# Moving eight U chunks from the one-hot table into the routing stage, and ending the expert gathers before the last V chunks

## The chip, the cores and the metric

One NeuronCore of a Trainium2 chip runs the whole layer in one launch. The metric is the device time of one execution in microseconds; the time before is the median of three runs. The engines are TensorE (PE, its weight loads shown as PEld), VectorE (DVE), ScalarE (ACT), GpSimd (POOL) and SyncE (SP), which only issues DMAs here.

## The reference, cut to what matters

The layer is attention plus a gated recurrence, followed by a product-key expert layer (PEER) and a last RMSNorm, for 512 tokens of width 1024. Nearly all of the change lies in PEER:

```python
sc = einsum('bshpd,phnd->bshpn', q, keys)          # 8 heads, 2 key halves, 128 keys each
v1, i1 = top_k(sc[..., 0, :], 16); v2, i2 = top_k(sc[..., 1, :], 16)
cand = v1[..., :, None] + v2[..., None, :]          # 256 candidates per head
best, pos = top_k(cand, 16); idx = take(i1 * 128 + i2, pos)   # 16 experts of 16384 per head
gates = softmax(best)
act = gelu(einsum('tkd,td->tk', u[idx], h))         # u, v: (16384, 1024)
out = einsum('tk,tkd->td', gates * act, v[idx])
```

## The kernel before, in words

The experts are done in two ways. For 352 tokens (`DT`) the kernel does not gather: it computes all 16384 activations and outputs densely, as 128 chunks of 128 experts. A **U chunk** (`act_pieces`, L629 on) loads 512 KB of `u`, splits it on ACT into `hi` (L142) and on DVE into `lo` (L162) so that two fast fp32 products replace a slow one, and does 24 matmuls of 352 columns (L646); ACT writes `gelu` of it to one of 53 held tiles (`KEEP`). A **V chunk** (the loop `for c in range(NE)` near the end) loads 512 KB of `v`, splits it likewise, multiplies the held tile by the gates (`w`, L980; `whi`, `wlo`, L985) and adds 18 matmuls of 512 columns (L994 to L996) to six accumulators. The other 160 tokens are done sparsely: 320 **gather steps** (128 for 128 tokens of block 0 with `u`, 32 and 32 for the other 32 tokens, 128 with `v`). Each is an indirect DMA issued by POOL (L707), 128 rows of 1024 floats into one of four tiles (`GB`), and one DVE instruction on it (L715 for `u`, L725 for `v`).

The stages after the front part are these.

1. **Routing.** Sixteen key halves (`hp`). Each loads its weights `wq` and keys, projects (24 matmuls of 512 columns), forms scores (L847) and takes the best 16 on DVE; every second one also runs `route` on DVE. `fill(int(F1 * (hp + 1)) - int(F1 * hp))` puts U chunks between the halves: with `F1 = 1.5` one and two in turn, 24 in all. Two more follow the routing.
2. **Table.** The gates must be spread to a dense table `G` of 128 x 128 experts by 352 tokens. For 22 slices of 16 tokens, DVE builds one-hot tiles `oh` (L904 to L907, two buffers), PE multiplies them (L912, 8 matmuls per group of 4 tokens, 88 groups), ACT copies out (L914) and issues the write to DRAM (L916, 1 MB per slice). After each group one quarter of a U chunk is put on PE (`piece`), until 48 chunks are held. `pace(goal, after)` issues gathers up to `goal` and puts the DVE step that lies three behind (`GLAG`) after the instruction named.
3. **Hold.** Three U chunks, two V loads, the first read of the table (`g_load`, which must wait for the last table write), nine gathers up to number 16 (`EARLY`), two U chunks.
4. **Loop.** 128 V chunks, the remaining 75 U chunks spread over the first 116 (`UEND`), and the remaining 304 gather steps, spread in proportion to the chunks done (`share`). Near the end `final_rows` adds the parts, normalises and writes out; block 0 of the tokens (`ys[0]`) is done after the loop.

The order on each engine is chosen by the tile scheduler from the order of the program, its priorities and the `issue_after` hints; POOL's gathers and the table's matmuls keep program order.

Of the kernel before, what the change touches and what calls it, by code (L numbers as in the profile page):

```python
# [6 lines left out]
F32 = mybir.dt.float32  # L7
# [5 lines left out]
OP = mybir.AluOpType  # L13
# [33 lines left out]
VPRE = 2  # L47
GLAG = 3
GB = 4
TAILC = 2  # L50
HELD = 5
LASTU = 2
EARLY = 16
UEND = 116
TL = 2
F1 = 1.5


def host(inp):
# [57 lines left out]
def layer(nc, tc, a, out, probe=None, upto=99):  # L117
# [37 lines left out]
    def wsplit(raw, shape, parts=1, eng=None):  # L155
        hi = oc.tile(list(shape), F32R, tag="hi", bufs=HB, name=nm("hi"))
        lo = oc.tile(list(shape), F32R, tag="lo", bufs=HB, name=nm("lo"))
        n = shape[1] // parts
        for i in range(parts):
            m = slice(i * n, (i + 1) * n)  # L160
            hi_of(hi[:, m], raw[:, m])
            (eng or V).tensor_tensor(lo[:, m], raw[:, m], hi[:, m].bitcast(F32), op=OP.subtract)  # L162
        return hi, lo


# [455 lines left out]
    with tc.tile_pool(name="peer", bufs=1) as pp, tc.tile_pool(name="psp", bufs=1, space=PSUM) as psp, ExitStack() as ps:  # L621
# [7 lines left out]
        def gel_tile(c):  # L629
            i = c % KEEP  # L630
            if i < LOOK:
                return pp.tile([P, DT], F32, tag="gel", bufs=LOOK, name=nm("gel"))
            if i < LOOK + LATE:
                return cur["gel2"].tile([P, DT], F32, tag="gel2", bufs=LATE, name=nm("gel"))
            return extra[i - LOOK - LATE]


        def act_pieces(c, pin=False):
# [237 lines left out]
        with tc.tile_pool(name="gb", bufs=1, reuse_waits="tile") as gp:  # L876
            iT = gp.tile([P, 2, DT], F16, name="iT")
            gs = gp.tile([P, DT], F32, name="gs")
            g16 = gp.tile([P, 2, DT], F16, name="g16")
            fill(2)  # L880
            for n in range(1, NB):
                f = X if n == 1 else 0
                t = slice((n - 1) * P - X + f, n * P - X)
                b = bank((P, 4, P))
                for w in range(2):
                    PE.transpose(b[:, w, :], i12[:, w, n, :], ident)
                PE.transpose(b[:, 2, :], gta[:, n, :], ident)
                ACT.activation(iT[:, :, t], b[:, 0:2, f:], AF.Copy)
                ACT.activation(gs[:, t], b[:, 2, f:], AF.Copy, scale=GS)  # L889
                V.tensor_copy(g16[:, 0, t], gs[:, t])  # L890
                V.tensor_tensor(g16[:, 1, t], gs[:, t], g16[:, 0, t], op=OP.subtract)
            NQ = OT // QT
            shape = [P, NQ, P, QT]
            for s_ in range(NPT):
                G_ = gp.tile([P, NE, TG], F32, tag="G", bufs=2, name=nm("G"))
                for o in range(TG // OT):
                    t = slice(s_ * TG + o * OT, s_ * TG + (o + 1) * OT)

                    def row(x):
                        return x.rearrange("p (q t) -> p q t", t=QT).unsqueeze(2).to_broadcast(shape)  # L900

                    ioq = iok.unsqueeze(1).to_broadcast(shape)
                    oh = gp.tile([P, 3, NQ, P, QT], F16, tag="oh", bufs=2, name=nm("oh"))
                    V.tensor_tensor(oh[:, 0], ioq, row(iT[:, 0, t]), op=OP.is_equal)  # L904
                    V.tensor_tensor(oh[:, 2], ioq, row(iT[:, 1, t]), op=OP.is_equal)
                    V.tensor_tensor(oh[:, 1], oh[:, 2], row(g16[:, 0, t]), op=OP.mult)
                    last = V.tensor_tensor(oh[:, 2], oh[:, 2], row(g16[:, 1, t]), op=OP.mult)  # L907
                    for q in range(NQ):
                        b = bank((P, QT, P))
                        for i in range(QT):  # L910
                            for w in range(2):
                                lastg = tc.keep_in_program_order(PE.matmul(b[:, i, :], oh[:, 0, q, :, i], oh[:, 1 + w, q, :, i], start=w == 0, stop=w == 1))  # L912
                        m = o * OT + q * QT
                        ACT.activation(G_[:, :, m:m + QT].rearrange("p c t -> p t c"), b, AF.Copy)  # L914
                        piece(KEEP - HELD)
                ACT.dma_start(Gd.rearrange("g p s f -> s p g f")[s_], G_.rearrange("p (g c) t -> p g (c t)", c=GC))  # L916
                pace((s_ + 1) // 3, last.ins)
        late = ps.enter_context(tc.tile_pool(name="late", bufs=1, reuse_waits="tile"))
# [17 lines left out]
                return SP.dma_start(gts[g], Gd[g])  # L936

        with tc.issue_after(lastg.ins):
            fill(KEEP - nu[0] - LASTU)
        for c in range(VPRE):  # L940
            v_load(c)
        g0 = g_load(0)
        pace(EARLY, last.ins)
        with tc.issue_after(lastg.ins), tc.issue_after(g0.ins):
            fill(LASTU)

# [22 lines left out]

        todo_u = NE - nu[0]  # L970
        nu0 = nu[0]
        ready = []
        for c in range(NE):
            if c % GC == 0:
# [38 lines left out]
            if c == NE - 6:  # L1013
# [4 lines left out]
                    bs.append(bank(tag="p"))  # L1018
                    PE.matmul(bs[hf][0:X, :], fold[:, 0:X], sp1.ax[:, hf * 512:(hf + 1) * 512], start=True, stop=True)
                final_rows(yx[0:X, :], [b[0:X, :] for b in bs], P, X)  # L1020
            pace(EARLY + (NS - EARLY) * share, last.ins)

        while nsp[0] < NS:
            sparse(nsp[0])
            nsp[0] += 1
        final_rows(ys[0], [sp0.ax[:, 0:512], sp0.ax[:, 512:]], 0, P)
        for n in range(DB):
            m = min(P, DT - n * P)
            final_rows(ys[n + 1][0:m, :], [acc[n][hf][0:m, :] for hf in range(2)], T0 + n * P, m)
# [17 lines left out]
```

## Time and profile before

| | before |
|---|---|
| median of 3 runs | 1669.36 us (1662.62 to 1670.48) |
| the profiled execution | 1675.46 us, its span 1673.7 us |
| PE busy | 1605.2 us (96%) |
| DVE busy | 1321.9 us (79%) |
| ACT, POOL busy | 709.6 us (42%), 487.3 us (29%) |
| moved by DMA | 400.87 MB, mean 240 GB/s |

The profiled execution was 6.1 us longer than the median of the timed runs. Busy shares are averages over stages with different limits, so they say little here: the stages are read one by one, from the stretches in the section of rows. A row of the timeline is start, duration, engine, line, operation, output and inputs; a bracket at its end tells how long the engine sat idle before it and what released it. A row of the stretches gives for each engine the busy time and the number of instructions, then TensorE's granted clock as a share of 2.4 GHz, the busy share of the 16 DMA engines and the rate.

### The profile page before, as it was taken

The numbers are of one execution on the slowest core, as the hardware profiler recorded it, in microseconds if no ns is written. First come the engines' busy times: TensorE is split into PE (matmuls) and PEld (weight loads), VectorE is DVE, ScalarE is ACT, GpSimd is POOL, SyncE is SP. The second block draws the span as 40 slices with busy tenths as digits, with TensorE's granted clock in tenths as the row PEclk, the third lists the DMA queues.
The fourth block names the chain that finished last, engine by engine and source line by source line (L and its number), as shares of the span: only waits on it lengthen the run. The fifth ranks groups of instructions, "written<-read, shape, count | busy, mean of one in ns | idle before, by whom it ended". The sixth has DMA issues, their size and how long they took to land.

```text
span 1673.7 us, 23435 instructions
## 1 busy us (share of the span) xinstructions
PE 1605.2 (96%) x8511; PEld 1358.7 (81%) x8511; DVE 1321.9 (79%) x2560; ACT 709.6 (42%) x1152; POOL 487.3 (29%) x341
## 2 busy tenths in 40 slices
PE   8999999999999969997899999999999999999996
PEld 6877678888988869997788888887888888888874
DVE  8456663647999988887688888878888888888887
ACT  5433353234554547775333333333333333333333
POOL 4000000000000010002455555445455555554542
PEclk9999999999999979999899999999999999999998
DMA  5311133334333347888999999999999999999984
GB/s 173 101 51 51 51 104 111 103 115 154 108 109 116 103 126 192 219 224 265 336 340 353 349 368 349 337 341 339 344 368 351 359 354 347 360 358 363 343 305 145
DMA packets 197491, 400.87 MB, mean 240 GB/s; under 512 B 103344, under 2 KB 105904, under 8 KB 197376
## 3 DMA queue, kind: packets, MB, share of 16 engines
q1 hardware_dynamic: 58832, 206.02, 35.2%
q0 software_dynamic: 46336, 168.39, 27.0%
q10 hardware_dynamic: 92208, 24.98, 6.1%
q8 instruction: 66, 1.08, 0.3%
q14 instruction: 49, 0.40, 0.1%
HBM read 371.91 MB, written 27.39 MB: 239 GB/s over the span
## 4 chain that ended last, share of the span: by engine, by line
PE 53%; issue 16%; POOL 12%; DVE 12%; DMA 6%; ACT 1%; POOLq 0%; DVEq 0%; SPq 0%; ACTq 0%
PE b L646 13%; POOL ga L707 11%; PE b L263 5%; PE b L262 5%; PE b L995 5%; PE b L996 5%; PE b L265 4%; PE b L994 4%; DMA ga<-v,idx 4%; PE b L912 4%; DVE lo L162 3%; DMA ga<-un,idx 1%; DVE ti L858 1%; DVE mr L856 1%; DVE e L725 1%
## 5 line engine op out<-in xcount | busy, mean ns | idle before, releaser
L707 POOL DMA_INDIRECT ga<-un,idx x160 | 225.2, 1407 | 944.5 <-ACT gs L889 581.3
L646 PE MATMUL b<-hT,hi 128*128 128x352 f32 x2048 | 366.9, 327 | 2.2 <-ACT hi L142 1.7
L646 PEld LDWEIGHTS b<-hT,hi 128*128 128x128 f32 x2048 | 334.4, 190 | 12.7 <-ACT hi L142 2.0
L995 PE MATMUL b<-lo,whi 128*128 128x512 f32 (+1 forms) x768 | 305.0, 397 | 15.0 <-DVE lo L162 14.6
L996 PE MATMUL b<-hi,wlo 128*128 128x512 f32 (+1 forms) x768 | 304.3, 396 | 0.0
L994 PE MATMUL b<-hi,whi 128*128 128x512 f32 (+1 forms) x768 | 302.7, 395 | 0.0
L707 POOL DMA_INDIRECT ga<-v,idx x160 | 240.4, 1502 | 208.3 <-DVE e L725 190.3
L142 ACT ACTIVATE hi<-s 128x1024 fp32r<-128x1024 f32 (+1 forms) x195 | 205.1, 1052 | 203.1 <-PE b L646 88.1
L162 DVE TENSOR_TENSOR lo<-s,hi 128x1024 fp32r<-128x1024 f32 (+1 forms) x195 | 238.5, 1224 | 29.7 <-ACT hi L142 28.0
L142 ACT ACTIVATE whi<-w 128x352 fp32r<-128x352 f32 x128 | 63.7, 498 | 400.0 <-PE b L995 361.2
L725 DVE SCALAR_TENSOR_TENSOR e<-ga,wt,e 128x1024 f32<-128x1024 f32 x158 | 202.2, 1280 | 19.3 <-DMA ga<-v,idx 18.4
L715 DVE SCALAR_TENSOR_TENSOR ga<-ga,h 128x1024 f32<-128x1024 f32 x160 | 194.5, 1220 | 28.6 <-DMA ga<-un,idx 26.9
L646 PE MATMUL b<-hT,lo 128*128 128x352 f32 x1024 | 191.3, 325 | 11.8 <-DVE lo L162 11.8
L995 PEld LDWEIGHTS b<-lo,whi 128*128 128x128 f32 (+1 forms) x768 | 138.8, 181 | 59.2 <-DVE lo L162 22.0
L646 PEld LDWEIGHTS b<-hT,lo 128*128 128x128 f32 x1024 | 168.0, 189 | 12.4 <-DVE lo L162 12.3
L996 PEld LDWEIGHTS b<-hi,wlo 128*128 128x128 f32 (+1 forms) x768 | 138.5, 180 | 39.3
L994 PEld LDWEIGHTS b<-hi,whi 128*128 128x128 f32 (+1 forms) x768 | 138.2, 180 | 35.3 <-ACT hi L142 1.2
L142 ACT ACTIVATE hi<-vr 128x1024 fp32r<-128x1024 f32 x128 | 134.6, 1051 | 75.9 <-PE b L646 46.3
L162 DVE TENSOR_TENSOR lo<-vr,hi 128x1024 fp32r<-128x1024 f32 x128 | 156.1, 1220 | 9.4 <-ACT hi L142 9.4
L263 PE MATMUL b<-hT,hi 128*128 128x512 f32 (+1 forms) x376 | 146.4, 391 | 0.3 <-DVE hT L145 0.3
L262 PE MATMUL b<-hT,hi 128*128 128x512 f32 (+1 forms) x376 | 146.1, 390 | 0.2
L985 DVE TENSOR_TENSOR wlo<-w,whi 128x352 fp32r<-128x352 f32 x128 | 67.0, 523 | 80.9 <-ACT whi L142 77.5
(284 smaller groups left out, 1960.5 us busy)
## 6 DMA issues: line engine op xcount, KB each, us to landing
s<-uc SPq DMA_DIRECT2D x128, 512.0 KB
vr<-vc SPq DMA_DIRECT2D x128, 512.0 KB
Gd<-G ACTq DMA_DIRECT2D x22, 1024.0 KB
gt<-Gd SPq DMA_DIRECT2D x32, 704.0 KB
s<-wfm SPq DMA_DIRECT2D x30, 512.0 KB
s<-wq SPq DMA_DIRECT2D x16, 512.0 KB
s<-wmg SPq DMA_DIRECT2D x8, 512.0 KB
s<-wout SPq DMA_DIRECT2D x8, 512.0 KB
```

The source lines that it names most:

```text
L142: ACT.activation(dst, src, AF.Copy)
L162: (eng or V).tensor_tensor(lo[:, m], raw[:, m], hi[:, m].bitcast(F32), op=OP.subtract)
L262: PE.matmul(b, wh[:, k, :], rh(i), start=start and i == 0, stop=False)
L263: PE.matmul(b, wh[:, k, :], rl(i), start=False, stop=False)
L646: m = PE.matmul(o, w[:, k, :], z[:, k, t], start=i == 0, stop=i == 3 * KD - 1)
L707: tc.keep_in_program_order(POOL.indirect_dma_start(out=t, out_offset=None, in_=a[src], in_offset=bass.IndirectOffsetOnAxis(ap=b.idx[:, j:j ...
L715: V.scalar_tensor_tensor(t, t, 1.0, h20, op0=OP.mult, op1=OP.mult, accum_out=b.act[:, j:j + 1])
L725: V.scalar_tensor_tensor(b.ax, t, b.wt[:, j:j + 1], b.ax, op0=OP.mult, op1=OP.add)
L985: last = V.tensor_tensor(wlo, w, whi.bitcast(F32), op=OP.subtract)
L994: PE.matmul(acc[tb][hf][0:m, :], whi[:, t], vh[:, d], start=i == 0, stop=False)
L995: PE.matmul(acc[tb][hf][0:m, :], whi[:, t], vl[:, d], start=False, stop=False)
L996: PE.matmul(acc[tb][hf][0:m, :], wlo[:, t], vh[:, d], start=False, stop=i == NE - 1)
```

## The change

Five constants and statements change. `F1 = 2.0` puts two U chunks behind every key half (32 instead of 24); so 34 are done when the table begins, and its 14 remaining chunks (56 quarters) are spread evenly over the 88 groups. The held tiles are taken in another order, since more of them are needed before the pool of the last 17 opens. In the hold, each of the three U chunks brings one gather, whose DVE step is put behind that chunk's `lo`; the burst up to number 16 goes, so the loop begins with 10 gathers issued and has 310 to issue. `TAILC = 8` makes `share` reach 1 at V chunk 119 (counted from 0) instead of 125, and the last steps and the end of block 0 are put into the loop at chunk 123.

```diff
-TAILC = 2
+TAILC = 8
-EARLY = 16
-F1 = 1.5
+F1 = 2.0
...
-            (eng or V).tensor_tensor(lo[:, m], raw[:, m], hi[:, m].bitcast(F32), op=OP.subtract)
+            cur["lo"] = (eng or V).tensor_tensor(lo[:, m], raw[:, m], hi[:, m].bitcast(F32), op=OP.subtract)
...
-            if i < LOOK + LATE:
-                return cur["gel2"].tile([P, DT], F32, tag="gel2", bufs=LATE, name=nm("gel"))
-            return extra[i - LOOK - LATE]
+            if i < LOOK + E8S:
+                return extra[i - LOOK]
+            return cur["gel2"].tile([P, DT], F32, tag="gel2", bufs=LATE, name=nm("gel"))
...
+            NPT_B = DT // QT
+            npc = 4 * (KEEP - HELD - nu[0])
...
-                        piece(KEEP - HELD)
+                        k = (s_ * TG + m) // QT
+                        if (k + 1) * npc // NPT_B > k * npc // NPT_B:
+                            piece(KEEP - HELD)
...
         with tc.issue_after(lastg.ins):
-            fill(KEEP - nu[0] - LASTU)
+            for _ in range(KEEP - nu[0] - LASTU):
+                fill(1)
+                pace(nga[0] + 1, cur["lo"].ins)
...
-        pace(EARLY, last.ins)
...
+        e0 = nga[0]
...
-            pace(EARLY + (NS - EARLY) * share, last.ins)
-
-        while nsp[0] < NS:
-            sparse(nsp[0])
-            nsp[0] += 1
-        final_rows(ys[0], [sp0.ax[:, 0:512], sp0.ax[:, 512:]], 0, P)
+            if c == NE - 5:
+                while nsp[0] < NS:
+                    sparse(nsp[0])
+                    nsp[0] += 1
+                final_rows(ys[0], [sp0.ax[:, 0:512], sp0.ax[:, 512:]], 0, P)
+            pace(e0 + (NS - e0) * share, last.ins)
```

How the order of instructions moves is shown at three places. Lines of the changed kernel lie a few off those before (L162 is L161 there, L715 is L714, L725 is L724, L960 is L964).

SP in the middle of the routing, which issues the loads of the keys (`ky`), the projection weights (`wq`) and the U chunks (`uc`). Before:

```order
L836 DMA ky_3902<-keys 128x128
L152 DMA s_660_3788<-uc 128x1024
L152 DMA s_665_3821<-uc 128x1024
L836 DMA ky_4052<-keys 128x128
L152 DMA s_682_3904<-wq 128x1024
L870 DMA gate_3082<-gta 32x32
L152 DMA s_688_3942<-uc 128x1024
L836 DMA ky_4206<-keys 128x128
```

Now:

```order
L835 DMA ky_3847<-keys 128x128
L151 DMA s_634_3666<-wq 128x1024
L151 DMA s_640_3704<-uc 128x1024
L151 DMA s_645_3737<-uc 128x1024
L835 DMA ky_4001<-keys 128x128
L151 DMA s_669_3849<-wq 128x1024
L151 DMA s_675_3887<-uc 128x1024
L151 DMA s_680_3920<-uc 128x1024
```

Between two loads of keys there stand one and two U chunks in turn before, and always two now.

DVE at the end of the table and in the hold, from the last one-hot tiles to the first weighted tile `w` of the loop (`ga` is a gathered tile, `act` its sums). Before:

```order
L907 TENSOR_TENSOR oh_7456<-oh_7456,g_5521 128x1024
L715 SCALAR_TENSOR_TENSOR ga_6902,act_3079<-ga_6902,h_62 128x1024
...
L162 TENSOR_TENSOR lo_7349<-s_1252_7346,hi_7348 128x1024
L715 SCALAR_TENSOR_TENSOR ga_7609,act_3079<-ga_7609,h_62 128x1024
...
L715 SCALAR_TENSOR_TENSOR ga_7624,act_3079<-ga_7624,h_62 128x1024
L162 TENSOR_TENSOR lo_7510<-s_1275_7507,hi_7509 128x1024
L162 TENSOR_TENSOR lo_7542<-s_1279_7539,hi_7541 128x1024
L162 TENSOR_TENSOR lo_7574<-s_1283_7571,hi_7573 128x1024
L980 SCALAR_TENSOR_TENSOR w_7708<-gel_3136,gt_7607 128x352
```

Now:

```order
L908 TENSOR_TENSOR oh_7450<-oh_7450,g_5779 128x1024
L161 TENSOR_TENSOR lo_7505<-s_1270_7502,hi_7504 128x1024
L714 SCALAR_TENSOR_TENSOR ga_6977,act_3079<-ga_6977,h_62 128x1024
L161 TENSOR_TENSOR lo_7541<-s_1276_7538,hi_7540 128x1024
L714 SCALAR_TENSOR_TENSOR ga_7196,act_3079<-ga_7196,h_62 128x1024
L161 TENSOR_TENSOR lo_7577<-s_1282_7574,hi_7576 128x1024
L714 SCALAR_TENSOR_TENSOR ga_7415,act_3079<-ga_7415,h_62 128x1024
L985 SCALAR_TENSOR_TENSOR w_7690<-gel_3136,gt_7614 128x352
```

The `...` stand for two and four more gather steps. Nine of them stood before the three held `lo`; now each `lo` comes first and one step follows it.

DVE at the end of the loop (`e_528` holds block 0's sums, `vr` is a raw V chunk). Before:

```order
L725 SCALAR_TENSOR_TENSOR e_528_3077<-ga_14917,wt_3080,e_528_3077 128x1024
L162 TENSOR_TENSOR lo_14957<-vr_14887,hi_14956 128x1024
L985 TENSOR_TENSOR wlo_14964<-w_14960,whi_14962 128x352
L725 SCALAR_TENSOR_TENSOR e_528_3077<-ga_14920,wt_3080,e_528_3077 128x1024
L985 TENSOR_TENSOR wlo_14974<-w_14970,whi_14972 128x352
L725 SCALAR_TENSOR_TENSOR e_528_3077<-ga_14953,wt_3080,e_528_3077 128x1024
L162 TENSOR_TENSOR lo_14967<-vr_14923,hi_14966 128x1024
L960 TENSOR_TENSOR e_2724_14751<-e_2724_14751,e_528_3077 128x512 x2
```

Now:

```order
L724 SCALAR_TENSOR_TENSOR e_528_3077<-ga_14709,wt_3080,e_528_3077 128x1024
L724 SCALAR_TENSOR_TENSOR e_528_3077<-ga_14742,wt_3080,e_528_3077 128x1024
L161 TENSOR_TENSOR lo_14790<-vr_14712,hi_14789 128x1024
L990 TENSOR_TENSOR wlo_14797<-w_14793,whi_14795 128x352
L964 TENSOR_TENSOR e_2733_14778<-e_2733_14778,e_528_3077 128x512
L985 SCALAR_TENSOR_TENSOR w_14872<-gel_14196,gt_14605 128x352
L964 TENSOR_TENSOR e_2733_14778<-e_2733_14778,e_528_3077 128x512
```

The last gather step stood before the `lo` of the very last V chunk; now seven `lo` of V chunks come after it.

## Rows read from the trace of the kernel before

**Rows 1.** The stretches: routing, table, hold, loop, end; times from the span's start.

```profile
391.60:580.30 188.70, 184.37 (x1014) 166.64 (x1013) 177.99 (x883) 102.43 (x224) 0.00 (x0) 1.00 0.35 116
611.50:783.30 171.80, 169.60 (x1227) 156.84 (x1226) 146.39 (x209) 118.65 (x128) 12.72 (x9) 0.99 0.78 213
783.30:818.67 35.37, 22.90 (x128) 22.18 (x127) 19.59 (x28) 11.05 (x15) 14.69 (x11) 0.86 0.96 328
818.67:1639.80 821.13, 810.18 (x4040) 686.68 (x4040) 697.29 (x895) 297.01 (x409) 427.85 (x304) 1.00 0.95 348
1639.80:1673.70 33.90, 19.27 (x71) 13.82 (x70) 22.43 (x34) 10.93 (x30) 9.90 (x1) 0.81 0.34 117
```

**Rows 2.** The timeline of PE in the routing, score matmuls of five key halves.

```profile
391.61 1.13 PE L847 MATMUL b<-ky,s 128*128 128x128 f32 x8
...
427.70 1.16 PE L847 MATMUL b<-ky,qp 128*128 128x128 f32 x8
441.82 1.16 PE L847 MATMUL b<-ky,qp 128*128 128x128 f32 x8
...
568.86 1.16 PE L847 MATMUL b<-ky,qp 128*128 128x128 f32 x8
580.30 1.16 PE L847 MATMUL b<-ky,qp 128*128 128x128 f32 x8 [0.84 <-ACT qp L844]
```

**Rows 3.** The timeline of PE in the loop: one U chunk, two V chunks.

```profile
1240.54 2.70 PE L646 MATMUL b<-hT,hi 128*128 128x352 f32 x16
...
1244.34 0.39 PE L994 MATMUL b<-hi,whi 128*128 128x512 f32 x1
...
1252.71 1.59 PE L646 MATMUL b<-hT,hi 128*128 128x352 f32 x9
```

**Rows 4.** The timeline of PE in the table: a group, a quarter chunk, a group.

```profile
619.36 1.12 PE L912 MATMUL b<-oh 128*128 128x128 f16 x8
620.24 1.20 PE L646 MATMUL b<-hT,lo 128*128 128x352 f32 x6
621.28 1.00 PE L912 MATMUL b<-oh 128*128 128x128 f16 x7
```

**Rows 5.** Groups by line, DVE in the table (612 to 781 us).

```profile
L904 DVE TENSOR_TENSOR oh<-iok,iT 128x1024 f16<-128x1024 f16 x43 | 29.7, 691 | 22.2 <-PE b L912 22.2
```

**Rows 6.** The timeline of DVE, PE and SP's queue in the hold.

```profile
789.58 1.23 DVE L715 SCALAR_TENSOR_TENSOR ga<-ga,h 128x1024 f32<-128x1024 f32 x1 [3.71 <-DMA ga<-un,idx]
...
799.72 2.71 PE L646 MATMUL b<-hT,lo 128*128 128x352 f32 x8 [10.75 <-DVE lo L162]
...
804.22 0.33 SPq L936 DMA_DIRECT2D gt<-Gd  x1
```

**Rows 7.** Who waited for the gathered tiles in the loop: us in total, times.

```profile
  POOL ga L707: 382.9, 285
  DVE e L725: 18.4, 20
  DVE ga L715: 15.6, 17
```

**Rows 8.** Two stretches of 20 us in the loop.

```profile
960.00:980.00 20.00, 20.00 (x104) 17.23 (x103) 17.01 (x26) 7.40 (x10) 11.53 (x9) 1.00 0.98 371
1480.00:1500.00 20.00, 18.55 (x94) 15.61 (x94) 15.96 (x18) 6.12 (x9) 8.93 (x7) 1.00 1.02 405
```

**Rows 9.** The timeline of POOL, DVE and PE at the end of the loop.

```profile
1639.79 9.91 POOL L707 DMA_INDIRECT ga<-v,idx  x1 [1.89 <-DVE e L725]
...
1653.36 1.28 DVE L725 SCALAR_TENSOR_TENSOR e<-ga,wt,e 128x1024 f32<-128x1024 f32 x1 [4.48 <-DMA ga<-v,idx]
1654.57 1.22 DVE L162 TENSOR_TENSOR lo<-vr,hi 128x1024 fp32r<-128x1024 f32 x1
...
1655.84 0.80 PE L995 MATMUL b<-lo,whi 128*128 128x512 f32 x1 [4.04 <-DVE lo L162]
...
1661.09 0.40 PE L995 MATMUL b<-lo,whi 128*96 128x512 f32 x1
```

## The prediction

> **What bounds the kernel now.** I read the stretches first [rows 1], since shares over the whole span mix five stages, and then the timeline and the waits of each stage.
>
> In the routing PE is busy for 184.37 of 188.70 us and DVE for 177.99: both are nearly full. In the table PE is busy for 169.60 of 171.80 us, DVE for 146.39. In the hold PE works for 22.90 of 35.37 us. In the loop PE is busy for 810.18 of 821.13 us, while the 16 DMA engines are busy for 0.95 of the time at 348 GB/s. In the end stretch the granted clock is 0.81 of 2.4 GHz and PE works for 19.27 of 33.90 us. So PE sets the pace nearly everywhere, and a gain can come only from places where it waits, or from work that it does there at a lower rate. The work itself stays: 128 U and 128 V chunks before and after.
>
> The price of a chunk on PE comes from the loop [rows 3]: a U chunk takes 1244.34 - 1240.54 = 3.80 us, two V chunks take 8.37, one 4.185.
>
> **The routing pays.** The time from one score group to the next [rows 2] is 14.12 us with two U chunks between them (427.70 to 441.82) and 11.44 with one (568.86 to 580.30); in the latter PE waits 0.84 us for ACT's copy of the projection. The fifteen intervals take 188.69 us and hold 22 chunks: seven have two, eight have one. Now all have two: 15 x 14.12 = 211.8, which is 23.1 us more. From the other side, eight chunks at the full 3.80 are 30.4 us, less the 4.3 us in which the stretch shows PE idle, so 26.1. DVE gains eight `lo` of 1.22 us [rows 9], 9.8 us, which lie under PE: 178.0 + 9.8 = 187.8 of some 212. ACT's eight copies and SP's eight loads of 512 KB lie under it too (DMA is busy for 0.35 of the stretch [rows 1]). I take **+24**, near the interval, because it is a duration from start to start. The Trainium skill (Perfetto Trace Analysis, Identifying the Most-Contended Engine) says that matmul busy time is no good measure of how full PE is; the two one-sided sums show it, and by busy time alone this term would be 26. The rest of the routing, from the last scores to the table, keeps its four U chunks and its DVE chain, so I cost it at nothing; what covers it is that PE's last scores, not DVE, start that chain.
>
> **The table gains.** One group of 8 matmuls takes 0.88 us from start to start, one quarter of a U chunk 1.04 [rows 4]; 88 x 1.92 = 169 us, the whole stretch. So PE sets this stage, and DVE waited 22.2 us for it to free a one-hot tile [rows 5]. With 56 quarters PE needs 88 x 0.88 + 56 x 1.04 = 135.7 us, 33.3 less. But then DVE is level: its 146.4 us less 8 x 1.22 is 136.6. Two engines with the same load, two buffers between them and quarters that come one or two per pair of groups do not run without waits; I add some 6%, which gives 144 to 145. I take **-25**, between -33 (no waits) and -18 (a slice of 7 us instead of 6.6). DMA is the third: busy for 0.78 of 171.8 us, 134 us, less eight loads; it fits into 145 us, narrowly.
>
> **The hold gains.** DVE runs in program order. Nine gather steps stood before the three `lo`, and DVE waited for their data (3.71 us at one of them); PE waited 10.75 us for the `lo` [rows 6]. Then SP could issue the first read of the table only at 804.22, 21 us after the table's end, because the last table write shared the DMA engines with those gathers; and the two U loads queued behind that read on SP came after it. Now three steps stand there, each behind its `lo`. Six gathers of 0.524 MB fewer are 3.15 MB: 7.8 us at the fastest 20 us of the trace (405 GB/s [rows 8]), 9.6 at the hold's own 328 [rows 1]. Five U chunks are 19.0 us of 35.4, so at most 16 can go; if the last write alone is what takes the time, nothing goes. I take **-8**. What is late next is the same read: PE has three U chunks and then waits for the fourth, some 7 us.
>
> **The loop pays.** It begins with 10 gathers instead of 16 issued, and the gathers end at V chunk 119 instead of 125. Per chunk of either kind that is 310/195 = 1.59 gathers instead of 304/201 = 1.51. A V chunk with a U chunk moves 0.524 + 0.180 (its share of the table) + 0.524 + 1.51 x 2 x 0.524 = 2.81 MB before and 2.89 now, in 7.985 us of PE: 352 and 362 GB/s, 2.9% more. That rate exists: 371 GB/s at a full PE in one stretch, 405 in another, where PE lost 1.45 us [rows 8]. DVE has 697 of 821 us [rows 1], some 15% free. PE's own time for 128 V and 75 U chunks is 820.7 us; it took from 818.67 to 1662.9 (1661.09 and eight more matmuls at 0.23 us), 844.3. Of the 23.6 lost, the end explains 6.5 (below), the loop 17. The lower bound of the extra loss is nothing (the 371 stretch), the upper 17 again, if loss grows as the idle share of the DMA engines halves from 0.05. I take **+4**, nearer to the full stretch, since DVE waited for gathered data for only 34 us in 37 places [rows 7].
>
> **The end gains.** The last gather was issued at 1639.79 and kept POOL for 9.91 us; DVE waited for it until 1653.36, and only then did the last `lo`; PE stood for 4.04 us [rows 9]. After that it ran at the lower level (1.2 GHz): the 12 matmuls from 1655.84 to 1661.09 took 5.25 us, against 2.79 at 4.185/18. Together 6.5 us. Now seven `lo` follow the last step. If the gather takes 13.6 us again, DVE stands, but PE has seven V chunks, 29 us, to make it up. The normalisation of the last rows stays behind PE's end either way. I take **-6**, between -3 (the same wait, half of it passed on) and -7.
>
> **Sum:** 24 - 25 - 8 + 4 - 6 = -11. The profiled execution took 1675.46 us and would take 1664; it stands 6 us above the median of the runs, and against that median, 1669.36, the forecast is **1658**. A measurement of this kernel can tell about 0.5%, 8.35 us, from no change.
>
> **The rivals.**
>
> *Gathers cannot come faster (slower).* The loop drew 304 gathers in 821.13 us, one per 2.70 [rows 1]. If four tiles and the DMA queues allow no more, 310 take 837 us, and the last eight V chunks (33.5 us) come after them: PE ends 870.8 us after the first V chunk instead of 844.3, +26.5 in place of +4 - 6. The sum is +17.5: 1687. It decides by the interval: above 2.67 us the change is slower by over 0.5%, below 2.62 faster; I count on 2.61. For it: POOL waited for DVE to free a tile 285 times [rows 7], and DMA is at 0.95. Against it: DVE rarely waited for the data, so it was the plan that held the gathers back, and 371 to 405 GB/s were drawn. The Trainium skill (DMA: Bandwidth & Descriptors, Specifications) gives some 358 GB/s as a core's limit from HBM; at today's busy share an estimate by it is 340 GB/s, and the 285 MB up to the last gather would take 837 us, the same 1687. The stretches at 371 and 405 disagree with it, which is why it gets little.
>
> *The moved chunks gain nothing (same).* The routing pays 30.4, all eight chunks in full, because DVE holds it up as well, and the table saves only 18 because DVE and the table writes hold it: 30.4 - 18 - 8 + 4 - 6 = +2, 1672. For it: DVE's 94% in the routing, and DVE level with PE in the table. Against it: 14.12 us is a measured interval with two chunks, DVE's work in it included.
>
> *Everything fits (faster still).* The table saves 33, the hold 12, the loop adds nothing: 24 - 33 - 12 - 6 = -27, 1642.
>
> **How the numbers follow.** The forecast as summed gets 0.56, gathers that come no faster 0.12, no gain from the moved chunks 0.21, everything fits 0.11. The forecast's own range, with each term at its bounds in turn, is 1648 to 1668; of its 0.56, 0.45 lie beyond 0.5% faster. So faster 0.45 + 0.11 = 0.56; the same 0.11 + 0.19 = 0.30; slower 0.12 + 0.02 = 0.14. The range for 8 in 10 goes from 1645 to 1674: it takes in the second rival and leaves out the first and the end of the third.
>
> **What would show it.** Right: score groups 14.1 to 14.3 us apart; the table about 145 us long with DVE and PE both above 90%; no wait of PE above 5 us for a `lo` in the hold, and the table's first read some 13 us after its end; the loop at 355 to 360 GB/s with PE's loss near 20 us; no gather beside the last seven V chunks, and PE's last matmuls at full clock. Wrong: intervals above 15 us, a table above 155 us, or DVE waiting for gathered data far beyond 34 us.

## The result, and the profile after

The changed kernel took 1680.61 us in the median of five runs (1676.73 to 1681.62), the kernel before 1663.72 (1662.62 to 1670.48): a ratio of 1.0077, with a 95% interval of 1.0048 to 1.0106. Later series gave 1676.37 against 1667.24, ratio 1.0066 (1.0042 to 1.009). So it is 0.7% **slower**, some 9 to 17 us; forecast were 11 us faster. The time lies outside the forecast's range of 1645 to 1674.

The profiled execution of before, 1675.46 us, turned out to be one of the longest of its kernel (the runs of before in the largest series spread from 1660.67 to 1675.74). So I took a second profile of each kernel ("again" below); the second of before took 1669.2 us, close to the median. The stages, in us:

| | before | before again | after | after again | predicted | again, after less before |
|---|---|---|---|---|---|---|
| routing, first to last score | 188.7 | 188.7 | 214.1 | 214.3 | +24 | **+25.6** |
| last score to table | 31.2 | 31.2 | 28.5 | 28.5 | 0 | **-2.7** |
| table | 172.0 | 171.9 | 147.7 | 148.0 | -25 | **-23.9** |
| hold | 35.4 | 35.7 | 34.2 | 34.5 | -8 | **-1.2** |
| first V chunk to PE's end | 844.3 | 837.0 | 851.6 | 849.6 | +4 - 6 | **+12.6** |

The last column sums to +10.4; the rows after PE's end are 1.2 us shorter.

The stretches of the changed kernel, from the view of stretches (columns as in [rows 1]): routing, table, hold, the loop up to 1600, and what follows the last gather.

```profile
392.93:607.01 214.08, 214.08 (x1204) 198.04 (x1204) 194.30 (x895) 112.95 (x240) 0.00 (x0) 1.00 0.36 121
635.46:783.13 147.67, 140.88 (x1036) 130.35 (x1035) 130.90 (x193) 97.52 (x109) 6.59 (x6) 0.97 0.80 212
783.13:817.30 34.17, 23.99 (x127) 23.42 (x126) 19.23 (x28) 13.74 (x18) 12.43 (x8) 0.85 0.92 310
817.30:1600.00 782.70, 763.65 (x3814) 648.83 (x3813) 669.09 (x858) 275.59 (x376) 423.97 (x299) 0.99 0.96 354
1624.96:1678.40 53.44, 43.64 (x182) 31.53 (x180) 36.89 (x55) 22.29 (x48) 1.41 (x1) 0.95 0.41 139
```

PE is without a gap in the routing, and near full in the table. In the loop it stands for 782.70 - 763.65 = 19.1 us up to 1600. The same stretch of the two profiles of before:

```profile
818.82:1600.00 781.18, 770.36 (x3874) 657.35 (x3873) 663.22 (x852) 280.91 (x383) 410.14 (x291) 1.00 0.95 350
```

```profile
819.89:1600.00 780.11, 769.92 (x3873) 656.91 (x3872) 663.24 (x852) 279.76 (x382) 410.75 (x291) 1.00 0.95 351
```

There PE stands for 10.8 and 10.2 us. Both kernels show idle times that repeat to within 1 us, so the 9 us between them belong to the kernels. Below, **idle** is always this: the stretch from the first V chunk to 1600, less PE's busy time in it. (A loop's **loss**, as in the prediction, is its whole time up to PE's end less the 820.7 us that PE needs for its work.)

Whom PE waits for there, and what DVE waits for, in the changed kernel (waits: us in total, times, longest):

```profile
DVE ga L714 <- DMA ga<-un,idx: 22.8, 30, 2.0
DVE e L724 <- DMA ga<-v,idx: 22.0, 29, 2.0
PE b L1000 <- DVE lo L161: 18.3, 20, 3.7
```

and in the kernel before:

```profile
DVE ga L715 <- DMA ga<-un,idx: 17.3, 19, 2.4
DVE e L725 <- DMA ga<-v,idx: 13.9, 19, 1.6
PE b L995 <- DVE lo L162: 10.5, 12, 3.2
```

PE waits for hardly anything in the loop but the `lo` of a chunk (18.7 of the 19.1 us), and DVE's waits for gathered tiles have grown from 31.2 to 44.8 us. One such place, from the timelines of DVE and PE in the changed kernel:

```profile
1408.36 1.28 DVE L724 SCALAR_TENSOR_TENSOR e<-ga,wt,e 128x1024 f32<-128x1024 f32 x1 [0.87 <-DMA ga<-v,idx]
1409.56 0.52 DVE L985 SCALAR_TENSOR_TENSOR w<-e,gt 128x352 f32<-128x352 f32 x1
1410.95 1.28 DVE L724 SCALAR_TENSOR_TENSOR e<-ga,wt,e 128x1024 f32<-128x1024 f32 x1 [0.87 <-DMA ga<-v,idx]
1412.15 1.22 DVE L161 TENSOR_TENSOR lo<-vr,hi 128x1024 fp32r<-128x1024 f32 x1
...
1413.42 0.51 PE L1000 MATMUL b<-lo,whi 128*128 128x512 f32 x1 [0.98 <-DVE lo L161]
```

DVE runs in order, and twice stands for a gathered tile; the `lo` behind it ends too late, and PE loses 0.98 us.

Idle is not the whole loss. The changed kernel's loop loses 851.6 - 820.7 = 30.9 us, of which 19.4 are idle, those after 1600 included. At PE's two longest waits, of 3.67 and 2.42 us, its granted clock was 0.50 (1.2 GHz) for 10.2 us in all. The first, from PE's timeline and the view of stretches:

```profile
1141.76 0.79 PE L1000 MATMUL b<-lo,whi 128*128 128x512 f32 x1 [3.67 <-DVE lo L161]
1142.35 0.63 PE L1001 MATMUL b<-hi,wlo 128*128 128x512 f32 x1
1142.78 0.63 PE L999 MATMUL b<-hi,whi 128*128 128x512 f32 x1
...
1140.30:1147.10 6.80, 5.34 (x13) 4.07 (x14) 5.10 (x8) 0.00 (x0) 2.99 (x3) 0.50 0.95 348
```

A matmul of a V chunk then comes every 0.43 us instead of 0.23 (4.185/18, from [rows 3]). That is some 5 us more; the other 6 lie in PE's busy time and were not traced to a cause. Before again had 3.4 us at 0.50 in its loop. This longest wait may not be a matter of gathers alone: some 10 us ahead of it DVE stood 2.02 us for the copies of `h` that the other 32 tokens need, and before and before again have their longest wait up to 1600 at the same place (3.15 and 2.65 us). That was not tried.

In the hold PE waits nearly as long as before (10.2 us for 12.5), but for another engine. ACT's and PE's timeline:

```profile
785.85 1.02 ACT L915 ACTIVATE G<-b 128x512 f32<-128x512 f32 x1 [5.48 <-DMA Gd<-G]
...
790.40 2.00 ACT L141 ACTIVATE hi<-s 128x1024 fp32r<-128x1024 f32 x2 [0.68 <-ACT gel L651]
791.51 4.65 PE L645 MATMUL b<-hT,hi 128*128 128x352 f32 x16 [7.42 <-ACT hi L141]
```

ACT's waits in the table (same columns as the waits above):

```profile
ACT G L915 <- DMA Gd<-G: 33.0, 14, 4.3
```

The kernel before has no such wait. Slices that come every 6.7 us instead of 7.8 find both `G` tiles still being written out (with the DMA engines busy for only 0.80 of the stretch), so ACT copies late, its last copies end after PE's last table matmuls, and the `hi` of the first held chunk stands behind them.

### The profile page after: what moved, and what is told of

Same layout as the page of the kernel before. It is cut to its first block, busy times and chain, and to the rows that moved or that the text cites. A ratio compares the mean times of both kernels' runs of the same rounds, so it can differ in the third digit from the quotient of the medians.

```text
span 1678.4 us, 23444 instructions
## 1 busy us (share of the span) xinstructions
PE 1611.5 (96%) x8511; PEld 1366.2 (81%) x8511; DVE 1326.9 (79%) x2560; ACT 700.5 (42%) x1152; POOL 479.0 (29%) x341
## 4 chain that ended last, share of the span: by engine, by line
PE 58%; DMA 17%; issue 9%; POOL 8%; DVE 4%; ACT 2%; POOLq 0%; DVEq 0%; SPq 0%; ACTq 0%
PE b L645 16%; DMA ga<-v,idx 8%; POOL ga L706 7%; DMA Gd<-G 6%; PE b L262 6%; PE b L261 6%; PE b L264 6%; PE b L1000 5%; PE b L1001 5%; PE b L999 5%; DVE lo L161 1%; ACT G L915 1%; DVE e L724 1%; PE b L913 1%; PE b L846 1%
## 5 line engine op out<-in xcount | busy, mean ns | idle before, releaser
L645 PE MATMUL b<-hT,hi 128*128 128x352 f32 x2048 | 366.0, 328 | 10.7 <-ACT hi L141 10.2
L645 PEld LDWEIGHTS b<-hT,hi 128*128 128x128 f32 x2048 | 337.6, 190 | 21.3 <-ACT hi L141 10.8
L706 POOL DMA_INDIRECT ga<-v,idx x160 | 229.4, 1434 | 196.2 <-DVE e L724 179.5
L161 DVE TENSOR_TENSOR lo<-s,hi 128x1024 fp32r<-128x1024 f32 (+1 forms) x195 | 238.6, 1224 | 49.1 <-ACT hi L141 44.3
L724 DVE SCALAR_TENSOR_TENSOR e<-ga,wt,e 128x1024 f32<-128x1024 f32 x158 | 202.3, 1280 | 25.1 <-DMA ga<-v,idx 22.0
L714 DVE SCALAR_TENSOR_TENSOR ga<-ga,h 128x1024 f32<-128x1024 f32 x160 | 194.3, 1220 | 25.1 <-DMA ga<-un,idx 22.8
L999 PEld LDWEIGHTS b<-hi,whi 128*128 128x128 f32 (+1 forms) x768 | 138.5, 180 | 35.4 <-ACT hi L141 1.2
L161 DVE TENSOR_TENSOR lo<-vr,hi 128x1024 fp32r<-128x1024 f32 x128 | 156.1, 1219 | 9.3 <-ACT hi L141 9.2
```

The costliest lines, as they stand in the source:

```text
L161: cur["lo"] = (eng or V).tensor_tensor(lo[:, m], raw[:, m], hi[:, m].bitcast(F32), op=OP.subtract)
L645: m = PE.matmul(o, w[:, k, :], z[:, k, t], start=i == 0, stop=i == 3 * KD - 1)
L706: tc.keep_in_program_order(POOL.indirect_dma_start(out=t, out_offset=None, in_=a[src], in_offset=bass.IndirectOffsetOnAxis(ap=b.idx[:, j:j ...
L714: V.scalar_tensor_tensor(t, t, 1.0, h20, op0=OP.mult, op1=OP.mult, accum_out=b.act[:, j:j + 1])
L724: V.scalar_tensor_tensor(b.ax, t, b.wt[:, j:j + 1], b.ax, op0=OP.mult, op1=OP.add)
L999: PE.matmul(acc[tb][hf][0:m, :], whi[:, t], vh[:, d], start=i == 0, stop=False)
```

## The experiments

I had two theories. **Full DMA engines:** the transfers have a ceiling near 355 GB/s, and denser gathers run into it. **Packed front:** the routing and table part does harm further on. A third came up on the way.

### The three parts apart

`e1`: only the routing and table part of the diff (`F1`, `gel_tile`, `npc`, `piece`). `e2`: only the hold part (`cur["lo"]`, one gather per held chunk, no burst to `EARLY`, `e0`). `e3`: only the end part (`TAILC`, last steps and block 0 at chunk 123). `e4`: all but the end part.

> Only the routing and table part on the kernel before: two U chunks per key half, 14 chunks spread over the table's 88 groups, the other order of the held tiles; hold, loop and end as before. **Full DMA engines** (the loop's long stretches can draw no more than some 355 GB/s, so the denser gathers are what costs): the two traces give +25.4 us in the routing, -2.7 from there to the table, -24.1 in the table, together -1.4; the hold with its nine gathers may lose some us more, since the table's writes now end later. Within 4 us of the kernel before, 1660 to 1668 by its median of 1663.7. **Packed front** (the loss comes from the routing and table part: DMA writes of the table are squeezed and run on into the hold and the loop): 8 to 17 us slower, 1672 to 1681.

> Only the hold part on the kernel before: each gather step of the hold behind its U chunk's lo, no burst up to number 16, so the loop begins with 10 gathers issued and does 310 up to V chunk 125. **Full DMA engines:** the hold gains 1 to 8 us, the loop has 2% more gathers per chunk (310/201 = 1.54 for 304/201 = 1.51) and loses 2 to 5 us: within 4 us of the kernel before. **Packed front:** the hold was only held up by the table's writes, and without them squeezed it gains its 8 us with a loop as before: 5 to 8 us faster.

> Only the end part on the kernel before: share reaches 1 at V chunk 119, last steps and block 0 at chunk 123, the burst up to 16 stays, so 304 gathers over 195 chunks (1.56 per chunk). **Full DMA engines:** the end gains 6.5 us, the loop pays for its gathers at some 355 GB/s: 1.56/1.51 is 3% more gathered bytes per chunk, 1.5% more bytes in all, some 12 us over the loop up to the last gather; 5 to 12 us slower than before, 1669 to 1676, with PE waits for late U and V chunks all over the loop. **Packed front:** the loop takes these gathers without loss, the end's 6.5 us are won: 5 to 7 us faster.

> The changed kernel without its end part: gathers up to V chunk 125 and block 0 after the loop, as before; routing, table and hold as changed. **Full DMA engines:** 310/201 = 1.54 gathers per chunk instead of 1.59, so most of the loop's loss goes, and the 6.5 us of the end come back: 1664 to 1672, 8 to 16 us faster than the changed kernel. **Packed front:** as slow as the changed kernel or slower by the end's 6.5 us, 1680 to 1687.

Measured against 35 runs of before (median 1667.21 us): e1 1670.08, ratio 1.0014 (0.9997 to 1.0031); e2 1665.68, 0.9988 (0.9968 to 1.0008); e3 1676.1, **1.0040** (1.0018 to 1.0062); e4 1669.81, 1.0021 (1.0002 to 1.0040). The end part is the one that costs for certain. The front by itself costs no more than 0.3%, so it does not explain the loss, though it takes away the hold's gain (below). In e4 PE's idle is 13.9 us, with the end part 19.

The hold and the loop of e2, as stretches:

```profile
780.38:806.34 25.96, 22.42 (x126) 21.83 (x126) 16.69 (x24) 11.18 (x15) 10.12 (x7) 0.93 1.00 336
806.34:1600.00 793.66, 778.28 (x3896) 662.36 (x3895) 673.85 (x870) 282.35 (x385) 419.46 (x297) 1.00 0.95 351
```

Alone, the hold part shortens the hold by 9.7 us, more than forecast. But the loop idles for 15.4 us instead of 10, and takes 845.2 us to PE's end instead of 837.0: the six gathers not done in the hold are done in the loop, at 310/201 = 1.54 per chunk, and the median moves by 1.5 us. In e1 the hold is longer than before:

```profile
780.41:821.49 41.08, 24.35 (x127) 23.77 (x127) 22.91 (x35) 13.59 (x18) 17.14 (x13) 0.79 0.96 325
```

41.1 against 35.7 us: that is what the squeezed table writes add behind the 1.6 us that the stages up to there save, and with the hold part on top it falls back to the 34 us of the changed kernel.

### Only the end of the gathers

```diff
-TAILC = 2
+TAILC = 8
```

> The kernel before with TAILC = 8 alone: the 304 gathers end at V chunk 119, block 0 is still finished after the loop. **Density** (the loop's loss grows with the gathers per chunk, 304/195 = 1.56 here): as the run with the whole end part, whose loop lost 26 us; 0.2 to 0.6% slower than before. **Place of block 0** (its two rows of additions and its normalisation beside the last V chunks are what cost there): no slower than before, or the end's 6.5 us faster.

1677.0 us, ratio 1.0057 (1.0033 to 1.0081), idle 17.3 us. So it is the packing of the gathers, not the place of block 0.

### Is there a ceiling?

`e5` takes two of three products of each V chunk away, with their `lo` and `wlo`.

> The changed kernel with only one of the three products in each V chunk (whi by hi): 6 matmuls instead of 18, and neither the lo nor the wlo of a V chunk on DVE. So PE's own time from the first V chunk on falls from 820.7 to some 465 us and DVE's by 190; every load, table read and gather stays. This leaves part of the output's sum out. **Full DMA engines:** the same 296 MB from the table's end to the last gather still need some 350 to 360 GB/s, 820 to 845 us: a time of 1620 to 1670, with PE idle half of the loop. **Engines in each other's way** (the loop's loss comes from DVE and PE running in order behind four gathered tiles, not from a ceiling of the transfers): the rate rises above 390 GB/s and the time falls below 1590.

1593.96 us, between the two theories' times. The stretch in the loop:

```profile
820.00:1480.00 660.00, 515.41 (x2426) 445.90 (x2425) 452.63 (x594) 272.11 (x372) 309.48 (x264) 0.89 1.00 388
```

The 16 DMA engines now are busy for 1.00 of the time and move 388 GB/s over 660 us. So there is a ceiling for this mix of transfers, but it lies 10% above the 354 GB/s that the changed loop draws, and "full DMA engines" is not the reason in the form I gave it.

### Less to gather, and gathers done earlier

`e6` leaves out every eighth step, transfer and DVE instruction both; `e7` is the hold part with 22 gathers in the table, `e10` with 29, `e8` is e7 with the end part.

```diff
-                pace((s_ + 1) // 3, last.ins)
+                pace(s_ + 1, last.ins)
```

> The changed kernel with every eighth gather step left out (40 of 320, each 0.524 MB and one DVE instruction), which leaves their part of the output out; PE's work stays. **Full DMA engines:** 21 MB fewer are 59 us of transfers at 355 GB/s, PE alone bounds the loop: its loss against 820.7 falls from 30.9 us to 10 or less, 18 to 28 us faster than the changed kernel, 1652 to 1662. **Packed order** (DVE's steps and the chunks' lo stand in an unlucky order at the start of the loop, whatever the rate): the loss falls only with the steps, an eighth of it, 4 us: 1674 to 1680.

> The kernel before with the hold part, and 22 instead of 7 gathers behind the table's slices (one per slice), so the loop has 295 left instead of 310. **Full DMA engines:** 15 gathers are 7.9 MB, 22 us of the later stages' transfers at 355 GB/s; the table has 0.22 of 172 us of its DMA engines free, 38 us, and DVE 25 us for 15 steps of 1.22. Hold and loop together fall by 10 to 20 us, the table grows by 0 to 6: 1650 to 1662. **Squeezed writes** (gathers beside the 256-byte packets of the table's writes slow these down, and the table or its first read comes later by as much): within 4 us of the kernel before, or slower, 1663 to 1680.

> The run before this one (hold part, 22 gathers in the table) with the end part as well: 295 gathers over 195 chunks, 1.51 per chunk, the density that the kernel before had. **Full DMA engines:** the room won by the early gathers is spent on ending them earlier: the end's 6.5 us are won, the loop loses 0 to 8: within 5 us of the run without the end part, 1648 to 1662. **The end part as such costs** (its place in the loop, the block 0 rows beside the last chunks): 7 us or more slower than the run without it.

> As the run with 22 gathers in the table, with 29 there instead; 288 left for the loop, 288/201 = 1.43 per chunk. **Density:** the loop, which lost 13 us at 1.47 and 2.9 at 1.38, loses 5 to 9; but the table's DMA engines (busy for 0.93 of it with 22) and DVE (157.8 of 171) are then full and it grows by 2 to 8: within 5 us of the run with 22, 1651 to 1661. **Free engines in the table:** the table stays at 171 us and the whole gain of the loop arrives: 1645 to 1651.

e6: 1648.74 us, idle 1.9. e7: **1656.16**, ratio 0.9935 (0.9912 to 0.9959), idle 9.1. e8: 1660.27, 0.9957 (0.9940 to 0.9974), idle 10.6. e10: 1660.03, 0.9953 (0.9938 to 0.9968), idle 5.1, but the table has grown from 170.6 to 175.3 us. e7's table:

```profile
608.64:779.20 170.56, 169.34 (x1227) 156.86 (x1227) 158.19 (x231) 118.78 (x128) 33.92 (x21) 0.99 0.93 256
```

The fifteen gathers more cost the table nothing; seven more still cost it 5 us. So the table had room, and e7 beats both kernels. e8 and e10 lie 4 us above e7, but their intervals overlap with its own.

The runs with four gathered tiles in which no gather is without its DVE instruction or the other way round (e17 is a control that comes further down), by steps left for the loop per chunk up to their end:

| steps per chunk | runs: idle of PE up to 1600, us |
|---|---|
| 270/195 = 1.38 | e6 (fewer steps in all): 1.9 |
| 288/201 = 1.43 | e10: 5.1 |
| 295/201 = 1.47 | e7: 9.1 |
| 1.51 | before: 10.8, again 10.2; e1: 8.3; e8: 10.6 |
| 310/201 = 1.54 | e2: 15.4; e4: 13.9 |
| 304/195 = 1.56 | e3: 16.4; e9: 17.3 |
| 310/198 = 1.57 | e17: 19.9 |
| 310/195 = 1.59 | after: 19.1, again 19.3 |

The idle time follows the density; at equal density the runs lie within 3 us of each other.

### Once more, for the spread

> The kernel before once more, for a second profile, since the profiled execution shown stands 8 us above the median of all runs. **Density:** routing, table and hold as in the first (188.7, 172, 35.4 us to within 1 us), and the difference lies in what the loop loses (23.6 us there): 10 to 18 us in an execution near the median. **Fixed stages vary:** the loop's loss is again 22 to 25 and the front stages are shorter.

> The changed kernel once more, for a longer series and a second profile. **Density:** 1.59 gathers per chunk, the most of all runs: the loop's loss again the largest, 27 to 35 us; the parts measured alone add up to 0.14 - 0.12 + 0.40 = 0.42%, and the hold part finds the hold held by the table's writes here, so 0.5 to 0.8% slower. **Chance of one execution:** a loss below 24 us and a ratio under 1.005.

Before again: the front stages repeat (table above), and the loop loses 837.0 - 820.7 = 16.3 us instead of 23.6, as "density" expected. Its end:

```profile
1640.52 1.21 POOL L707 DMA_INDIRECT ga<-v,idx  x1 [1.89 <-DVE e L725]
...
1652.00 0.50 PE L995 MATMUL b<-lo,whi 128*128 128x512 f32 x1 [0.30 <-DVE lo L162]
```

The last gather keeps POOL for 1.21 us, not 9.91, and PE waits 0.30 us, not 4.04 [rows 9]. In e1, e2, e4, e7 and e10 too, it took 1.05 to 1.21 us, and PE waited for 0.46 us at most near the end. The 9.91 us were an accident of one execution.

After again: ratio 1.0066, loss 849.6 - 820.7 = 28.9 us, idle 19.3, as "density" expected.

### Transfer or instruction?

`e13` keeps the DVE instruction of every eighth step and drops its transfer; `e14` the other way round.

> The changed kernel with every eighth gather's transfer left out, its DVE instruction kept (on the tile gathered before it), so that those experts' rows are not the right ones. **Transfers** (late data of a nearly full DMA make PE wait): as with both left out, PE idle for 1 to 5 us up to 1600, 1646 to 1656. **Steps** (DVE's instructions in order ahead of a chunk's lo make PE wait): as the changed kernel, idle 15 to 20, 1668 to 1680.

> The changed kernel with the DVE instruction of every eighth gather left out, its transfer kept, so that those experts' part of the output is missing. **Transfers:** nearly as the changed kernel, idle 13 to 20, 1668 to 1680. **Steps:** idle 1 to 6, 1646 to 1658.

e13: 1656.62 us, idle 6.1: most of the loss goes with the transfers. e14: **1717.25 us**, idle 44.7, against what either theory said. Its waits in the loop:

```profile
POOL ga L707 <- DMA ga<-un,idx: 80.2, 18, 11.4
POOL ga L707 <- DMA ga<-v,idx: 72.8, 25, 6.7
DVE e L727 <- DMA ga<-v,idx: 48.1, 31, 4.8
PE b L1003 <- DVE lo L161: 43.4, 26, 8.6
DVE ga L717 <- DMA ga<-un,idx: 43.1, 29, 4.4
```

and the stretch:

```profile
815.60:1600.00 784.40, 739.66 (x3647) 625.27 (x3646) 600.87 (x777) 263.84 (x360) 384.14 (x287) 0.98 0.92 339
```

A tile that no instruction reads is free here only when its own transfer has landed, so POOL waits for that, and the gathers behind it are issued late. DVE has fewer instructions, the DMA engines are less busy (0.92) and move less (339 GB/s), and yet PE loses more than twice as much. This speaks against both theories, and for a third: what counts is not how full anything is, but how long before its use a gather is issued. The trace of e13 has the time from a gather's issue to its landing:

```profile
DMA to landing us min/median/max: 4.2/7.3/11.5
```

A gather's DVE step stands three steps behind (`GLAG`), and POOL waited 260 times in the changed kernel's loop up to 1600 for a DVE step to free a tile. In the changed kernel 295 gathers in 782.70 us (the other four of POOL's 299 instructions copy `h`) are one per 2.65 us: three intervals are 8.0 us, hardly more than the median time to land. In e6 they are 3 x 784.78/264 = 8.9 us. This is the third theory, **lead**.

### A fifth tile

```diff
-LATE = 17
+LATE = 14
-GLAG = 3
-GB = 4
+GLAG = 4
+GB = 5
```

`e15` is this on the changed kernel, `e17` its control (`LATE = 14` alone), `e16` this on e7, `e18` on the kernel before. The space comes from three held tiles, so three U chunks move into the loop: 3 x 3.80 = 11.4 us of PE there, for some 7 us off the table (140.6 in e15, 147.7 in the changed kernel).

> The changed kernel with five gathered tiles instead of four and each DVE step four behind its gather, paid for with 14 instead of 17 late held tiles (three U chunks more in the loop, 1.6 MB). **Lead** (a gather is used about three intervals after its issue, 7.8 us at 2.61, and lands after 7.3 in the median and up to 12): four intervals are 10.4 us, so DVE hardly waits and PE's idle time up to 1600 falls from 19 us to 8 or less; 10 to 20 us faster than the changed kernel, 1658 to 1668. **Full DMA engines:** idle stays at 15 to 20, 1672 to 1684.

> The control for the run before: the changed kernel with 14 instead of 17 late held tiles and four gathered tiles as now. Both theories: three U chunks move from the table to the loop, the table gets shorter by up to 8 us and the loop longer by 11.4 us of PE; within 5 us of the changed kernel, 1672 to 1684, idle 17 to 23.

> The run with the hold part and 22 gathers in the table, with five gathered tiles and 14 late held tiles. **Lead:** its idle time of 9 us up to 1600 falls to 4 or less, 4 to 9 us faster than with four tiles, 1646 to 1653. **Full DMA engines:** no gain, or 2 to 5 us lost by the three chunks moved into the loop: 1655 to 1662.

> The kernel before with five gathered tiles and 14 late held tiles. **Lead:** its idle time of 10.5 us up to 1600 falls to 4 or less; 4 to 10 us faster than before, 1656 to 1663. **Full DMA engines:** no gain, 1665 to 1672.

Against before (median 1666.17): e15 **1654.75 us**, 0.9923 (0.9900 to 0.9946); its control e17 1681.73, 1.0107 (1.0080 to 1.0134); e16 1655.7, 0.9934 (0.9911 to 0.9958); e18 1661.91, 0.9975 (0.9964 to 0.9987). The fifth tile, with its DVE step one place later, takes 27 us from its control. e17 came out where both theories had it, with an idle of 19.9 us. e16 missed what lead forecast for it, 1646 to 1653, though its idle of 3.9 us is the one that lead forecast. The loops of e17 and e15 as stretches:

```profile
804.51:1600.00 795.49, 775.58 (x3889) 661.37 (x3888) 676.59 (x868) 280.95 (x383) 428.44 (x302) 0.99 0.95 351
810.32:1600.00 789.68, 784.94 (x3982) 674.21 (x3982) 683.76 (x881) 287.70 (x393) 456.93 (x307) 1.00 0.96 359
```

The waits in that of e15:

```profile
PE b L1000 <- DVE lo L161: 4.7, 4, 2.0
...
DVE ga L714 <- DMA ga<-un,idx: 3.2, 5, 1.5
DVE e L724 <- DMA ga<-v,idx: 1.8, 4, 0.8
```

And from the view of the gathered tile, the time from issue to landing, in e17 and in e15:

```profile
DMA to landing us min/median/max: 4.7/7.6/11.0
DMA to landing us min/median/max: 4.6/7.8/11.2
```

The rate is higher than in the control (359 GB/s for 351) and a gather takes no less time to land, but DVE waits for tiles for 5.0 us instead of 41.8 and PE idles for 4.7 instead of 19.9. Three intervals of 2.67 us are 8.0 us in e17; four of 2.61 are 10.5 in e15, near the longest landing. The rows say the same when each gather is set beside its own DVE step: from a gather's issue to the moment when DVE is ready for it there pass 8.7 us in the median in e17, and 55 of 298 gathers land after that moment; in e15 it is 10.8 us, and 9 of 302. (In before and in the changed kernel the medians are 8.8 and 8.6, with nine in ten above 7.6 and 6.6; their traces have no landings.) Lead is shown; full DMA engines is refuted. The tile and the place of the step were changed together, and which of the two gives the lead was not tried.

On before the same tile takes the idle from 10.5 to 2.1 us, worth 4.3 us in all. e16 lies within 2 us of e15 and of e7: with PE nearly without gaps, the early gathers and the fifth tile no longer add up, and e16 pays for the three U chunks in the loop (836.6 us to PE's end, for 833.8 in e7).

## Why the prediction was wrong

Of the five terms of the sum, routing and table held. Hold, loop and end failed: forecast were -8 + 4 - 6 = -10, measured -1.2 + 12.6 = +11.4.

**Routing, +24: right** (25.6). The intervals average 214.08/15 = 14.27 us; 14.12 was forecast. Of the two sums the one by busy time, 26.1, came nearer than the one by intervals, 23.1, which the working preferred: PE has no gap left in this stretch.

**From the last scores to the table, nothing: nearly right** (-2.7), as PE's wait for DVE's routing chain went from 11.42 to 7.92 us.

**Table, -25: right** (-23.9), with some luck: the 6% for waits was a guess, PE's busy time came to 140.9 us instead of 135.7, and its gaps to 6.8. But the step that called the third resource, DMA, a narrow fit costed it in the table alone. It did not fit: ACT waited 33.0 us for table writes, which PE saw only after the table.

**Hold, -8: wrong in the changed kernel** (-1.2). The term held for its own edit (e2: -9.7), and failed because it was summed with a table whose writes now end behind PE's work; e1 shows +5.4 in the hold from that. The read of the table was not late next, ACT's copies were. Nor would the gain have stayed: "what is late next" was looked for in the hold, while the gathers taken out of it came back in the loop (e2 as a whole: 0.9988).

**End, -6: wrong.** The working took 4.04 us of waiting and 2.5 of the lower clock from [rows 9] as what every execution pays. A 9.91 us row on POOL beside a group of 304 whose others take 1 to 2 us should have been read as an outlier. The term is 0: in before again the granted clock was 1.00 from 1640 us to PE's end, not 0.81.

**Loop, +4: wrong** in size, and the term that failed most. Since the end gave nothing, the +12.6 in the last row of the table are all the loop's: 9 of idle, the rest in PE's busy time, where the lower clock counts for 2. The density alone makes the kernel before 0.57% slower (e9). The sum had no term for the clock at a wait in the loop, though it priced one at the end. The bounds reached to +17, and I went to the lower end "since DVE waited for gathered data for only 34 us in 37 places". Those places were the mechanism, seen from the wrong side: a wait of DVE is passed on to PE at the next `lo`, and where gathers land about when they are needed, packing them 5% more densely nearly doubled PE's idle. The stretches of 371 and 405 GB/s [rows 8] told rightly that the rate exists; the rate was not what was short.

**The rivals.** "Gathers cannot come faster" had the right sign, and named the four tiles, but not the mechanism: by its own test, the interval, it fell: the last gather was issued 807.7 us after the first V chunk, 2.61 us for each of the 310, as the forecast counted on, and below the 2.67 that decides. The gathers did come faster, and PE paid for it. "The moved chunks gain nothing" fell too (routing 25.6, not 30.4; table -23.9, not -18), and "everything fits" as well (neither -33 in the table nor -12 in the hold). The Trainium skill's limit of some 358 GB/s (DMA: Bandwidth & Descriptors, Specifications), by which this rival was also priced, is passed by 388 in e5 over 660 us; the same page (Bandwidth, Measured) reports 425 GB/s for one core with the other idle, and only with both at work about 358 each. No run here has a second core at work. The same skill (Perfetto Trace Analysis, Optimization Strategy) says that a gap which keeps coming back on the engine that should be full can mean too few buffers; e15 agrees, with 19.1 us of gaps falling to 4.7.

What stays open: some 6 of the 30.9 us that the changed loop loses are neither idle nor the lower clock; why the landing times spread from 4 to 12 us was not tried, nor a sixth tile, nor a third `G` tile, for which there was no room beside the held tiles.

## What to carry to other kernels

For a pipelined fetch, compare the lead (buffers ahead times the interval between fetches) with the spread of the time to land, not only the rate with a ceiling: if the two are near each other, packing the fetches a few per cent more densely costs the consumer, and one buffer more, with the use set one place later, can turn the sign of a change (e15 against e17: 27 us). Work taken out of one stage is gained only if the stage that gets it has room; add the terms by stage with the resources that run on across the border (here the table's writes). And a gain read from a single long row should be checked against the other rows of its group, or a second profile.

## What was not expected of the hardware

- A gathered tile that nothing reads makes POOL wait for its own transfer's landing, 153.0 us in 43 places, and made the kernel some 40 us slower than the changed one while it did less (e14).
- Where PE waited longest in the loop, its clock was granted at 0.50 for 10.2 us in all, some 5 us of a loss that a sum of waits does not count; with the fifth tile (e15) the loop had none of it.
- With PE's work reduced, one core's DMA engines drew 388 GB/s over 660 us of mixed 512 KB loads and gathers (e5).
- Routing and table of one kernel repeat to within 0.4 us in its two profiles, while the start of the first score group varies from 388.6 to 392.9 us over the runs, and one gather's 9.91 us on POOL moved an end by some 7 us.
